# Low parts of three weight operands of the first feed-forward projection: an adding transfer in SBUF in place of a VectorE subtraction

## The chip, the cores and the metric

The kernel runs on one core of one Trainium2 chip. The metric is the device time of one execution in microseconds (us); the median of the runs counts. Engines are named as in the profile: PE is TensorE (its matmuls; PEld are its weight loads), DVE is VectorE, ACT is ScalarE, POOL is GpSimd, SP is SyncE, whose queue issues nearly all transfers.

## The reference, cut to what matters

One encoder layer over 2048 tokens of width 1024: windowed attention with a sink, then a SwiGLU feed-forward network of hidden width 2816, each between two RMS norms with shift, scale and gate from a conditioning vector. The change concerns the first product of the feed-forward network, `h @ w_in`.

```python
def swiglu(h, w_in, w_out):
    a, b = jnp.split(h @ w_in, 2, axis=-1)
    return (jax.nn.silu(a) * b) @ w_out

# in the layer:
    h = rmsnorm(x, ffn_norm_pre[i]) * (1.0 + sc2) + sh2
    y = swiglu(h, ffn_w_in[i], ffn_w_out[i])
    x = x + g2 * rmsnorm(y, ffn_norm_post[i])
```

All data is float32.

## The kernel before, in words

**Precision.** PE multiplies in a rounded format (`F32R`). To keep float32 accuracy each operand is held as a high part, the rounded value, and a low part, the operand less its high part. `three` (L876) issues three matmuls for one product: high by high, high by low, low by high. `split` (L882) makes the parts of an operand: ACT copies the operand into the rounded tile (`act.copy(hi, src)`), and then DVE subtracts (`lo = src - hi`).

**The first projection.** The tokens are done in two halves of 1024 (`hf`), and in each half the 44 column tiles of `w_in` in 22 pairs (`t`): the tile of `a` and that of `b` that belong together. One pair in one half is a `Hidden` block (L1540), so there are 44. A block is a 2 by 2 matrix product done by a scheme of seven products in place of eight. Its constructor, `Block.__init__` (L1490), loads the two weight tiles into `raw` (named `wiri` in the profile, 512 KB each), takes four quarters `a11, a12, a21, a22` from them, makes four sums and differences on DVE (`s1, s2, s4` as tiles of their own, `s3` over `a21`), and splits the seven operands `a11, s2, a12, s3, s1, a22, s4` into seven `w` tiles (L1511 to L1514), each of two times 128x512 elements. The profile names the tiles of `a11, a12, a22` together `wa_i`, those of the others `ws_i`. `step(i)` (L1518) then issues the 12 matmuls of one of the seven products (four slices of the contraction by `three`), 84 in a block. The activations' operands (`hb`, `ht`) are split once for each half.

**What comes of a product.** `take` (L1545) brings each product from its PSUM bank into the tiles `p1, u2, u3, b1`, on ACT for the first and on DVE for the others; ACT applies silu, POOL multiplies, and the results go to DRAM by SP for the second projection.

**Buffers.** There are two weight pools, used by even and odd blocks. Each has one `raw` tile and seven `w` tiles (`wbufs = 7`, L1458), so that operand `i` of block `t + 2` takes the place of operand `i` of block `t` once PE has used it.

**Order of the work.** No order is written by hand. `Recorder` (L142) records every operation with the regions that it reads and writes (`record`, L184) and a cost (`cost`, L256), and `schedule` (L702) makes the order of all engines from that: 18 rounds of a list schedule whose priorities come from a backward pass, of which it takes the one that does best under drawn lateness of transfers. So a change of one operation's cost or engine can move instructions everywhere, the attention included. What stands on an engine or a queue runs in its order; SP issues the transfers of loads and stores alike. All instructions are issued at one line of `emit`, L767 before and L771 after the change, so the profile is read by tile names.

**Around the start of the projection.** The last attention blocks store their output (`of`) to DRAM (`o_d`), from which the output projection of the last quarter of the tokens loads it as `ol`; its weights are `wo`. The first blocks' weights, the operands `hb` and `ht` and the normed activations (`y`, stored as `h2_d`, `hd_d`) are loaded, stored and split at the same time.

Of the kernel before, what the change touches and what calls it, by code (L numbers as in the profile page):

```python
# [16 lines left out]
AF = mybir.ActivationFunctionType  # L17
ALU = mybir.AluOpType
# [6 lines left out]
KT = D // P  # L25
# [116 lines left out]
class Recorder:  # L142
# [41 lines left out]
    def record(self, eng, fn, args, kw):  # L184
        op = Op()
        op.i, op.eng, op.fn, op.args, op.kw, op.ins = len(self.ops), eng, fn, args, kw, None
        aps = [(j, x) for j, x in list(enumerate(args)) + list(kw.items()) if isinstance(x, bass.AP)]
        out = {0}
        if fn == "custom":
            out = {1}  # L190
        elif fn == "tensor_tensor_reduce":
            out = {0, 7}
        elif fn == "activation" and "accum_out" in kw:
            out = {0, "accum_out"}
        op.writes = [self.region(x) for j, x in aps if j in out]
        op.reads = [self.region(x) for j, x in aps if j not in out]
        op.tiles = []
        if fn == "matmul" and not kw.get("start"):
            op.reads.append(op.writes[0])
        elif fn == "matmul" and op.writes[0][0].group is None:  # L200
            op.writes = [(op.writes[0][0], (3, (1 << P) - 1))]
        outs, ins = [x for j, x in aps if j in out], [x for j, x in aps if j not in out]
        op.forms, op.calls, op.stamp = {}, {}, 0
        for op.eng, op.fn, op.args, op.kw in (*self.others(eng, fn, args, kw, ins), (eng, fn, args, kw)):
            self.cost(op, outs, ins)
            op.forms[op.eng] = op.occ, op.lat, op.port, op.table
            op.calls[op.eng] = op.fn, op.args, op.kw
        op.eng_first = eng
        op.pred = {}
        for w, items in ((False, op.reads), (True, op.writes)):  # L210
            for b, m in items:
                for q, qw, qm in b.log:
                    if (w or qw) and q is not op and qm[0] & m[0] and qm[1] & m[1]:
                        op.pred[q] = max(op.pred.get(q, 0), self.gap(q, op))
        for w, items in ((False, op.reads), (True, op.writes)):
            for b, m in items:
                if w:
                    b.log = [e for e in b.log if not (e[2][0] | m[0] == m[0] and e[2][1] | m[1] == m[1]) or e[0] is op]
                b.log.append((op, w, m))
                if b.tag is not None and op not in b.ops:  # L220
                    if not b.ops:
                        b.tag.order.append(b)
                    b.ops.add(op)
                    op.tiles.append(b)
        if eng == "pe" and op.writes[0][0].group is not None:
            for q in op.writes[0][0].group:
                op.pred.setdefault(q, 0)
            op.writes[0][0].group = [op]
        op.succ = []
        for q in op.pred:  # L230
            q.succ.append(op)
        self.ops.append(op)
        return op
# [22 lines left out]
    def cost(self, op, outs, ins):  # L256
        fn, eng = op.fn, op.eng
        op.port, op.table, op.bytes = False, None, 0
        n = int(np.prod(outs[0].shape[1:])) if fn != "custom" else P
        sbuf = [x for x in ins if self.bufs[x.tensor.name].pool.space == "sbuf" and int(np.prod(x.shape[1:])) > 1] \  # L260
            if eng != "sp" else []
        psum = any(self.bufs[x.tensor.name].pool.space == "psum" for x in ins) if eng != "sp" else False
        if eng == "sp":
            op.bytes = int(np.prod(outs[0].shape)) * 4
            parts, run = outs[0].ap[0][1], min(self.run(x) for x in outs + ins)
            op.wire = op.bytes / (345.0 if run >= 2048 and parts == P else 270.0)
            op.occ, op.lat = 650 if parts == DH or run * 2 * P == op.bytes else 385 if run >= 2048 else 450, 0
            op.out = self.bufs[outs[0].tensor.name].pool.space == "dram"
        elif eng == "pe":
            if fn == "transpose":  # L270
                op.occ, op.lat = 108, 330
            elif outs[0].dtype == F32 and ins[0].dtype == F32:
                op.occ, op.lat = max(860 * n // CH, 230), max(1060 * n // CH, 400)
            else:
                op.occ = n * 0.4167 + 13.5
                op.lat = op.occ + 162
        elif eng == "act":
            op.occ = n / 1.2 + (51 if psum else 93)
            op.lat = op.occ + 105
            if fn == "activation":  # L280
                for more, ns in (("accum_out" in op.kw, 105), (isinstance(op.kw.get("scale"), bass.AP), 95),
                                 (isinstance(op.kw.get("bias"), bass.AP), 95)):
                    if more:
                        op.occ, op.lat = op.occ + ns, op.lat + ns
                f_ = op.args[2]
                op.table = {AF.Silu: "silu", AF.Ln: "log", AF.Exp: "log"}.get(f_)
        elif eng == "dve":
            fast = fn in ("tensor_copy", "tensor_scalar") and not psum
            op.occ = n / (1.92 if fast else 0.96) + 66
            op.lat = op.occ + 88  # L290
            if fn == "reciprocal":
                op.occ, op.lat = 90, 174
            if fn in ("tensor_tensor_reduce", "scalar_tensor_tensor") and any(
                    isinstance(x, bass.AP) and int(np.prod(x.shape[1:])) == 1 for x in op.args):
                op.occ, op.lat = op.occ + 62, op.lat + 62
            if fn == "tensor_tensor_reduce":
                op.lat += 84
            if outs[0].ap[0][1] == DH and fn == "tensor_tensor":
                op.occ, op.lat = op.occ + 97, op.lat + 10
            op.port = n > P and (fast or len(sbuf) > 1)  # L300
        else:
            op.port = fn != "custom"
            if fn == "tensor_tensor":
                op.occ = n * 2.21 + 125
                op.lat = op.occ + 45
            elif fn == "custom":
                op.occ, op.lat = 1000, 1050
            else:
                op.occ = n * 1.05 + 153
                op.lat = op.occ + 35  # L310
# [461 lines left out]
def f(ap):  # L772
    return ap.bitcast(F32)
# [14 lines left out]
def encoder_layer(ctx, tc, a):  # L788
# [697 lines left out]
    class Block:  # L1486

        STEPS = tuple(zip(("a11", "s2", "a12", "s3", "s1", "a22", "s4"), OPERANDS))

        def __init__(self, ops, i, u, wa, wb, keep=None, kept=None):  # L1490
            self.ops, self.u, m = ops, u, ops.m
            pl = wi[i % len(wi)]
            if kept:
                self.w = {}
                for n, _ in self.STEPS:
                    self.w[n] = w = pl.tile([P, 2, m, P], F32R, tag="w", bufs=wbufs, name=f"w{n}_{u}")
                    sp.dma_start(f(w), kept[n])
                return
            raw = pl.tile([P, 2, 2 * m, P], F32, tag="raw", name=f"wir{u}")
            sp.dma_start(raw[:, 0], wa)  # L1500
            sp.dma_start(raw[:, 1], wb)
            a11, a12, a21, a22 = [raw[:, i].rearrange("p (k e) c -> p e k c", e=2)[:, e] for i in range(2) for e in range(2)]
            sm_ = {n: pl.tile([P, m, P], F32, tag=n, name=f"{n}_{u}", bufs=1) for n in ("s1", "s2", "s4")}
            sm_["s3"] = a21
            dve.tensor_tensor(sm_["s1"], a21, a22, ALU.add)
            dve.tensor_tensor(sm_["s2"], sm_["s1"], a11, ALU.subtract)
            dve.tensor_tensor(sm_["s3"], a11, a21, ALU.subtract)
            dve.tensor_tensor(sm_["s4"], a12, sm_["s2"], ALU.subtract)
            src = dict(sm_, a11=a11, a12=a12, a22=a22)
            self.w = {}  # L1510
            for n, _ in self.STEPS:  # L1511
                w = pl.tile([P, 2, m, P], F32R, tag="w", bufs=wbufs, name=f"w{n}_{u}")
                split(w[:, 0], w[:, 1], src[n], dve)
                self.w[n] = w  # L1514
                if keep:
                    sp.dma_start(keep[n], f(w))
# [22 lines left out]

    class Hidden(Block):  # L1540
        def __init__(self, half, t, hf):
            super().__init__(half, t, f"i{half.u}_{t}", a["w_in"][t], a["w_in"][HT + t])
            self.t, self.got, self.hf = t, {}, hf

        def take(self, i, ps):  # L1545
# [377 lines left out]
```

## Time and profile before

| what | before |
|---|---|
| runs (us) | 2015.1, 2017.34, 2016.28; median 2016.28 |
| span of the profiled execution (us) | 2014.1 |
| PE busy (us, share of the span) | 1999.9, 99% |
| DVE busy | 1687.7, 84% |
| ACT busy | 1076.7, 53% |
| POOL busy | 559.6, 28% |
| DMA engines' mean busy share by packets of the main queue | 59.3% |
| matmuls | 9484 |

The profile gives the profiled execution by its span, from the first to the last instruction; a time of its own beside that is not given. The median of the runs lies 2016.28 - 2014.1 = 2.2 us above the span, the three runs 1.0 to 3.2 us above it. Busy times overlap, so they don't add up to the span. A matmul is recorded from its start to its modelled end, while the next starts before that end.

### The profile page before, as it was taken

The numbers are of one execution on the slowest core, as the hardware profiler recorded it, in microseconds if no ns is written. First come the engines' busy times: TensorE is split into PE (matmuls) and PEld (weight loads), VectorE is DVE, ScalarE is ACT, GpSimd is POOL, SyncE is SP. The second block draws the span as 40 slices with busy tenths as digits, with TensorE's granted clock in tenths as the row PEclk, the third lists the DMA queues.
The fourth block names the chain that finished last, engine by engine and source line by source line (L and its number), as shares of the span: only waits on it lengthen the run. The fifth ranks groups of instructions, "written<-read, shape, count | busy, mean of one in ns | idle before, by whom it ended". The sixth has DMA issues, their size and how long they took to land. (4 is left out here: it accounts for less than half of the span.)

```text
span 2014.1 us, 29137 instructions
## 1 busy us (share of the span) xinstructions
PE 1999.9 (99%) x9484; PEld 1675.3 (83%) x9484; DVE 1687.7 (84%) x3047; ACT 1076.7 (53%) x2100; POOL 559.6 (28%) x521
## 2 busy tenths in 40 slices
PE   9999999999999999999999999999999999999999
PEld 7888888888888788888888888888888888878888
DVE  7959888777989999988889988776676789989996
ACT  6657766777888863444343533333333744455433
POOL 0202433444757414332323211111111000130034
PEclk9999999999999999999999999999999999999999
DMA  9877655486788775444546833423323794398543
GB/s 350 303 281 279 225 201 188 171 302 218 239 290 288 270 274 177 172 174 157 193 161 230 286 128 126 142 89 110 110 95 126 244 322 150 113 322 302 174 155 111
DMA packets 208724, 415.23 MB, mean 206 GB/s; under 512 B 20107, under 2 KB 62140, under 8 KB 205500
## 3 DMA queue, kind: packets, MB, share of 16 engines
q1 hardware_dynamic: 208572, 413.37, 59.3%
q8 instruction: 75, 1.23, 0.3%
q14 instruction: 77, 0.63, 0.1%
HBM read 278.52 MB, written 134.77 MB: 205 GB/s over the span
## 5 line engine op out<-in xcount | busy, mean ns | idle before, releaser
L767 PE MATMUL bank<-ht,ws_i 128*128 128x512 f32 x1584 | 373.7, 389 | 0.0
L767 PEld LDWEIGHTS bank<-ht,ws_i 128*128 128x128 f32 x1584 | 297.4, 188 | 61.6
L767 PE MATMUL bank<-hb,wa_i 128*128 128x512 f32 x1056 | 255.2, 389 | 0.0
L767 PEld LDWEIGHTS bank<-hb,wa_i 128*128 128x128 f32 x1056 | 198.6, 188 | 41.2
L767 PE MATMUL bank<-ol,wo 128*128 128x512 f32 x768 | 207.2, 398 | 2.5 <-ACT ol L767 1.9
L767 DVE TENSOR_TENSOR u_i<-bank,u_i 128x512 f32<-128x512 f32 x176 | 120.8, 687 | 80.2 <-PE bank L767 79.2
L767 ACT ACTIVATE pr<-pr,nm 128x385 f32<-128x385 f32 (+1 forms) x256 | 154.8, 606 | 51.0 <-DVE nm L767 47.8
L767 ACT CAST ws_i<-s_i 128x512 fp32r<-128x512 f32 x132 | 82.0, 621 | 183.7 <-PE bank L767 147.2
L767 DVE CUSTOM_DVE_ANT_0 pr<-bank,bias,nsink 128x384 f32<-128x384 f32 (+1 forms) x256 | 150.0, 594 | 23.4 <-PE bank L767 19.6
L767 POOL TENSOR_SCALAR pr<-pr,rs 128x384 f32<-128x384 f32 (+1 forms) x184 | 116.6, 646 | 184.3 <-DVE rs L767 173.0
L767 PEld LDWEIGHTS bank<-ol,wo 128*128 128x128 f32 x768 | 142.4, 189 | 30.0 <-ACT ol L767 2.4
L767 POOL TENSOR_TENSOR p_i<-p_i,u_i 128x512 f32<-128x512 f32 x34 | 55.4, 1630 | 306.8 <-DVE u_i L767 187.8
L767 POOL TENSOR_TENSOR z<-z,z 128x512 f32<-128x512 f32 x31 | 49.6, 1611 | 327.3 <-DVE z L767 216.9
L767 PE MATMUL bank<-hi,ws 128*128 128x512 f32 x384 | 135.9, 399 | 0.0
L767 ACT CAST wa_i<-wiri 128x512 fp32r<-128x512 f32 x132 | 81.2, 620 | 101.0 <-PE bank L767 96.2
L767 DVE TENSOR_TENSOR plo<-bank,phi 128x512 fp32r<-128x512 f32 x184 | 121.1, 684 | 14.9 <-ACT phi L767 13.4
L767 PE MATMUL bank<-k,q 128*128 128x384 f32 (+1 forms) x512 | 132.7, 343 | 0.4 <-DVE nm L767 0.4
L767 PE MATMUL bank<-ht,wa_i 128*128 128x512 f32 x528 | 127.3, 389 | 0.0
L767 PE MATMUL bank<-hb,ws_i 128*128 128x512 f32 x528 | 127.1, 389 | 0.0
L767 DVE TENSOR_TENSOR z<-bank,z 128x512 f32<-128x512 f32 (+1 forms) x164 | 107.8, 659 | 16.9 <-PE bank L767 15.7
L767 ACT CAST phi<-bank 128x512 fp32r<-128x512 f32 x184 | 101.9, 587 | 29.0 <-PE bank L767 27.7
L767 DVE TENSOR_TENSOR wa_i<-wiri,wa_i 128x512 fp32r<-128x512 f32 x132 | 99.7, 756 | 20.9 <-ACT wa_i L767 20.9
(289 smaller groups left out, 4441.6 us busy)
## 6 DMA issues: line engine op xcount, KB each, us to landing
wiri<-w_in SPq DMA_DIRECT2D x88, 512.0 KB, 4.5
ada<-ada_w SPq DMA_DIRECT2D x38, 512.0 KB, 7.1
q_d<-e SPq DMA_DIRECT2D x32, 512.0 KB, 3.4
q<-q_d SPq DMA_DIRECT2D x16, 1024.0 KB, 6.8
wo<-wo_d SPq DMA_DIRECT2D x16, 1024.0 KB, 7.2
wiro<-w_out SPq DMA_DIRECT2D x40, 384.0 KB, 4.3
g_d_b<-p_i SPq DMA_DIRECT2D x44, 256.0 KB, 2.9
g_d_t<-p_i SPq DMA_DIRECT2D x40, 256.0 KB, 2.0
```

The costliest lines, as they stand in the source:

```text
L767: o.ins = getattr(engs[o.eng], o.fn)(*args, **kw)
```

## The change

For the three operands of a `Hidden` block that are plain quarters of the weights (`a11`, `a12`, `a22`), the low part is made in another way. ACT writes the high part as before. ACT also writes the operand times -1 into the low half of the tile, where it is rounded like the high part, so that it holds the negative high part. Then POOL issues a transfer from SBUF to SBUF that adds the operand to what the low half holds. The other four operands, and the blocks of the second projection, are split as before.

So that each quarter is one piece of 2 KB in a partition, the host lays `w_in` out with the even slices of the contraction first and the odd ones behind (`whole=True` selects the matching view). The recorder learns that such a transfer also reads what it writes, and it is costed at 1100 ns of POOL and 4500 ns to landing, without the port that POOL shares with DVE.

```diff
         if fn == "matmul" and not kw.get("start"):
+            op.reads.append(op.writes[0])
+        elif kw.get("accum_op") is not None:
             op.reads.append(op.writes[0])
...
-            op.port = fn != "custom"
-            if fn == "tensor_tensor":
+            op.port = fn not in ("custom", "dma_start")
+            if fn == "dma_start":
+                op.occ, op.lat = 1100, 4500
+            elif fn == "tensor_tensor":
...
-            a11, a12, a21, a22 = [raw[:, i].rearrange("p (k e) c -> p e k c", e=2)[:, e] for i in range(2) for e in range(2)]
+            form = "p (e k) c -> p e k c" if whole else "p (k e) c -> p e k c"
+            a11, a12, a21, a22 = [raw[:, i].rearrange(form, e=2)[:, e] for i in range(2) for e in range(2)]
...
-                split(w[:, 0], w[:, 1], src[n], dve)
+                if whole and n in ("a11", "a12", "a22"):
+                    act.copy(w[:, 0], src[n])
+                    act.activation(w[:, 1], src[n], AF.Copy, scale=-1.0)
+                    pool.dma_start(f(w[:, 1]), src[n], accum_op=ALU.add)
+                else:
+                    split(w[:, 0], w[:, 1], src[n], dve)
...
-            super().__init__(half, t, f"i{half.u}_{t}", a["w_in"][t], a["w_in"][HT + t])
+            super().__init__(half, t, f"i{half.u}_{t}", a["w_in"][t], a["w_in"][HT + t], whole=True)
...
-        "w_in": tiles(ffn_w_in[0]),
+        "w_in": tiles(ffn_w_in[0])[:, :, list(range(0, KT, 2)) + list(range(1, KT, 2))],
```

In the order of the instructions, 132 subtractions leave DVE (three for each of 44 blocks), and 132 activations on ACT and 132 transfers on POOL are new. The rest of the order is planned anew, and differs from the attention's first blocks on. Three places show it; a name such as `wa11_i0_0` is operand a11 of block 0 in the first half (`i1` is the second half), and the last number of a name only counts tiles.

PE, from the end of the attention to the first use of `ol3_3`, the last piece of attention output that is loaded; before, with three matmuls on `ol2_1` between the last attention product and the first row shown:

```order
L767 MATMUL bank1<-ol2_2_6066,wo2_7_7046 128x512 x6
L767 MATMUL bank1<-ol2_3_6097,wo2_7_7046 128x512 x6
L767 MATMUL bank0<-ol3_0_6624,wo3_0_7264 128x512 x6
L767 MATMUL bank0<-ol3_1_6924,wo3_0_7264 128x512 x6
L767 MATMUL bank0<-ol3_2_7231,wo3_0_7264 128x512
L767 MATMUL bank1<-ol3_0_6624,wo3_1_7367 128x512 x2
L767 MATMUL bank3<-hb110_0_7342,wa11_i0_0_7330 128x512
L767 MATMUL bank0<-ol3_2_7231,wo3_0_7264 128x512 x5
L767 MATMUL bank1<-ol3_0_6624,wo3_1_7367 128x512 x4
L767 MATMUL bank1<-ol3_1_6924,wo3_1_7367 128x512 x6
L767 MATMUL bank1<-ol3_2_7231,wo3_1_7367 128x512 x6
L767 MATMUL bank0<-ol3_3_7398,wo3_0_7264 128x512
```

The same stretch of PE after, with eleven matmuls on `ol2_0` and `ol2_1` between the last attention product and the first row shown:

```order
L771 MATMUL bank0<-ol2_2_6043,wo2_7_7110 128x512 x6
L771 MATMUL bank0<-ol2_3_6081,wo2_7_7110 128x512 x6
L771 MATMUL bank1<-ol3_0_6562,wo3_0_7240 128x512 x6
L771 MATMUL bank1<-ol3_1_6878,wo3_0_7240 128x512
L771 MATMUL bank0<-ol3_0_6562,wo3_1_7328 128x512 x2
L771 MATMUL bank1<-ol3_1_6878,wo3_0_7240 128x512 x4
L771 MATMUL bank3<-hb110_0_7346,wa11_i0_0_7338 128x512
L771 MATMUL bank1<-ol3_1_6878,wo3_0_7240 128x512
L771 MATMUL bank1<-ol3_2_7208,wo3_0_7240 128x512 x6
L771 MATMUL bank0<-ol3_0_6562,wo3_1_7328 128x512 x4
L771 MATMUL bank0<-ol3_1_6878,wo3_1_7328 128x512 x2
L771 MATMUL bank1<-ol3_3_7367,wo3_0_7240 128x512
```

With the matmuls named ahead of them, 52 matmuls stood between the last attention product and the first use of `ol3_3`; now 50 do. The first product that needs the low part of `wa11_i0_0` follows 21 matmuls behind that use.

POOL at the same time, before (`pr` is the attention's softmax, `y` and `yacc` belong to the norms):

```order
L767 TENSOR_SCALAR pr15_3_7111<-pr15_3_7111,rs15_3_7214 128x256 x4
L767 TENSOR_TENSOR y1_1_5399<-y1_1_5399,nx1_7150 128x512
L767 TENSOR_TENSOR y1_2_5559<-y1_2_5559,nx1_7150 128x512
L767 TENSOR_TENSOR y1_5_5977<-y1_5_5977,nx1_7150 128x512
L767 TENSOR_TENSOR y1_3_5676<-y1_3_5676,nx1_7150 128x512
L767 TENSOR_TENSOR y1_4_5793<-y1_4_5793,nx1_7150 128x512
L767 TENSOR_TENSOR y1_6_6000<-y1_6_6000,nx1_7150 128x512
L767 TENSOR_TENSOR yacc2_6299<-yacc2_6299,ysq2_7_7383 128x512
```

And after:

```order
L771 TENSOR_SCALAR pr15_3_7101<-pr15_3_7101,rs15_3_7153 128x256 x4
L771 TENSOR_TENSOR yacc2_6247<-yacc2_6247,ysq2_5_7223 128x512
L771 TENSOR_TENSOR y1_0_5285<-y1_0_5285,nx1_7264 128x512
L771 TENSOR_TENSOR y1_1_5397<-y1_1_5397,nx1_7264 128x512
L771 DMA wa11_i0_0_7338<-wiri0_0_6099 128x512
L771 TENSOR_TENSOR yacc2_6247<-yacc2_6247,ysq2_6_7311 128x512
L771 TENSOR_TENSOR y1_2_5538<-y1_2_5538,nx1_7264 128x512
L771 DMA wa12_i0_0_7362<-wiri0_0_6099 128x512
L771 TENSOR_TENSOR y1_5_5966<-y1_5_5966,nx1_7264 128x512
L771 TENSOR_TENSOR y1_4_5830<-y1_4_5830,nx1_7264 128x512
L771 TENSOR_TENSOR y1_7_6173<-y1_7_6173,nx1_7264 128x512
L771 TENSOR_TENSOR yacc2_6247<-yacc2_6247,ysq2_7_7379 128x512
```

The first two of block 0's three transfers stand among the norms of the second quarter, the third behind them. On SP, six transfers stood between the store of the last attention output and the load of `ol3_3`; now two do.

ACT in the middle of the second half (blocks 8 to 10), before:

```order
L767 COPY p1_i1_8_12480<-bank3 128x512
L767 CAST wa11_i1_10_12486<-wiri1_10_12312 128x512
L767 CAST ws2_i1_10_12502<-s2_i1_10_12378 128x512
L767 CAST wa12_i1_10_12520<-wiri1_10_12312 128x512
L767 ACTIVATE p1_i1_8_12480<-p1_i1_8_12480 128x512
```

And after:

```order
L771 COPY p1_i1_8_12575<-bank7 128x512
L771 ACTIVATE wa11_i1_10_12581<-wiri1_10_12435 128x512
L771 CAST wa11_i1_10_12581<-wiri1_10_12435 128x512
L771 CAST ws2_i1_10_12598<-s2_i1_10_12488 128x512
L771 ACTIVATE wa12_i1_10_12617<-wiri1_10_12435 128x512
L771 CAST wa12_i1_10_12617<-wiri1_10_12435 128x512
L771 ACTIVATE p1_i1_8_12575<-p1_i1_8_12575 128x512
```

In both, operand a11 of block 10 is copied directly behind the first product of block 8, which frees its tile; the new activation with -1 stands ahead of the copy. On SP, `wiri1_10` is loaded after block 8's a22 is done in both, after the change behind the landing of that block's three transfers.

More of the change, by code (lines that the diff above doesn't have):

```diff
@@ L1488, in encoder_layer, with __init__ @@
         STEPS = tuple(zip(("a11", "s2", "a12", "s3", "s1", "a22", "s4"), OPERANDS))
-        def __init__(self, ops, i, u, wa, wb, keep=None, kept=None):
+        def __init__(self, ops, i, u, wa, wb, keep=None, kept=None, whole=False):
             self.ops, self.u, m = ops, u, ops.m
```

## The prediction

> **What bounds the kernel now.** I read the page's busy times first, then the busy times stretch by stretch.
>
> ```profile
> core 0: us, PE busy (x) PEld busy (x) DVE busy (x) ACT busy (x) POOL busy (x), PEclk, DMA share, GB/s
> 100.00:650.00 550.00, 548.88 (x2902) 471.92 (x2901) 452.37 (x1095) 405.62 (x921) 241.15 (x292) 1.00 0.72 244
> ...
> 690.00:695.00 5.00, 2.54 (x9) 1.54 (x8) 2.79 (x4) 3.50 (x5) 0.68 (x1) 0.91 1.03 400
> 695.00:700.00 5.00, 5.00 (x18) 3.78 (x17) 4.00 (x6) 4.46 (x7) 0.00 (x0) 0.75 1.06 403
> 700.00:1560.00 860.00, 860.00 (x3796) 712.35 (x3795) 704.56 (x1040) 342.38 (x569) 206.39 (x135) 1.00 0.47 163
> ```
>
> The first projection runs from about 685 to 1564 us. Between 700 and 1560 PE is busy for all 860.00 us, at a granted clock of 1.00, with 3796 matmuls: one each 226.6 ns. Busy alone would not show a gap shorter than the overlap of two matmuls, so I looked for one in the pace:
>
> ```profile
> 1000.00:1050.00 50.00, 50.00 (x222) 41.40 (x222) 41.91 (x63) 21.91 (x34) 12.71 (x8) 1.00 0.49 166
> 1400.00:1450.00 50.00, 50.00 (x223) 41.40 (x222) 34.03 (x52) 15.84 (x26) 7.55 (x5) 1.00 0.29 101
> ```
>
> At 1000 us DVE is busy for 41.91 of 50 us, at 1400 us for 34.03, and the pace of PE is the same, 222 and 223 matmuls. So DVE sets nothing there. In the whole projection PE waits in one place, near its start. The waits of PE between 685 and 745 us, and the timeline around them:
>
> ```profile
> PE bank L767 <- ACT ol L767: 1.9, 1, 1.9
> PE bank L767 <- DVE ol L767: 0.5, 1, 0.5
> ```
>
> ```profile
> 678.05 0.42 PE L767 MATMUL bank<-plo,v 128*128 128x512 f32 x1
> ...
> 680.26 0.53 SPq L767 DMA_DIRECT2D o_d<-of  x1
> ...
> 684.78 0.32 SPq L767 DMA_DIRECT2D ol<-o_d  x1
> ...
> 691.14 1.04 ACT L767 CAST ol<-ol 128x1024 fp32r<-128x1024 f32 x1 [1.41 <-DMA ol<-o_d]
> ...
> 692.23 0.73 PE L767 MATMUL bank<-ol,wo 128*128 128x512 f32 x2 [1.93 <-ACT ol L767]
> ```
>
> The last attention product starts at 678.05, its output is stored at 680.26 and loaded again at 684.78, and ACT can copy it at 691.14; PE, out of other work, waits. From 690 to 700 us it does 9 + 18 = 27 matmuls where 10 us at 226.6 ns hold 44, in part at a clock of 0.75: 17 x 0.2266 = 3.9 us are lost. That is all the time near the change that can be won.
>
> **The change, part by part.** Rows of the operand tiles, then the group on the page:
>
> ```profile
> L767 ACT CAST wa_i<-wiri x132: 602/622/642, 678.1 to 1529.1; 128x512 fp32r<-128x512 f32 x132
> ```
>
> ```profile
> L767 DVE TENSOR_TENSOR wa_i<-wiri,wa_i 128x512 fp32r<-128x512 f32 x132 | 99.7, 756 | 20.9 <-ACT wa_i L767 20.9
> ```
>
> DVE loses 132 x 756 ns = 99.8 us. It lies wholly beside PE's 860.00 of 860 us, so it is worth 0; what is late next, with DVE gone, is PE itself, as it is now. ACT gains 132 copies with a factor; the nearest row is its plain copy, 622 ns, so 82 us on an engine that is busy for 342.38 of 860 us. It stays below half; 0. If that cover were gone, 82 us would be the price.
>
> POOL gains 132 issues. No transfer issued by POOL is in the trace. The nearest row is SP's issue of the same weights (327/423/1841 ns):
>
> ```profile
> L767 SPq DMA_DIRECT2D wiri<-w_in x88: 327/423/1841, 580.1 to 1492.7; - x88
> ```
>
> By these ends it is 43 to 243 us in all; I take the upper one, since POOL must make the transfer's list in some way, and 206 + 243 still leaves half of 860 us idle. Queued behind a POOL transfer that waits for ACT are POOL's products of the gated halves; they go to DRAM and are used a phase later. So 0.
>
> The landing is what a matmul now waits for. Transfers of the steady part, and of the crowded start (680 to 745 us):
>
> ```profile
> wiri<-w_in SPq DMA_DIRECT2D x36, 512.0 KB, 4.5
> g_d_t<-p_i SPq DMA_DIRECT2D x18, 256.0 KB, 2.0
> ```
>
> ```profile
> DMA packets 11364, 22.99 MB, mean 354 GB/s; under 512 B 1248, under 2 KB 1504, under 8 KB 11360
> ...
> ht<-hd_d_t SPq DMA_DIRECT2D x16, 256.0 KB, 5.8
> ...
> wor<-w_o SPq DMA_DIRECT2D x4, 512.0 KB, 6.8
> ```
>
> An adding transfer of 256 KB reads its source and its target, so it lies between the copy of 256 KB and of 512 KB: 2.0 to 4.5 us steady, 5.8 to 6.8 us at the start. I take the upper ends. The Trainium skill (Collectives: The Full Stack, "The bandwidth ceiling: the fold count and why AG ≠ RS ≠ AR") says that the adding itself is free, but that two sources are read, which makes twice the read traffic of a copy; it speaks against the change, and the sum by it is the upper end, by a plain copy the lower. No run of before shows such a transfer.
>
> How early it starts is told by the order of the instructions: operand i of block t + 2 is written when operand i of block t has been used. A block has 84 matmuls, 19.0 us, a product 12, 2.7 us. So from there to its own use lie 2 x 19.0 - 2.7 = 35.3 us, for two ACT operations (1.2 us), POOL's issue (1.8 at most) and the landing (4.5): 28 us of reserve. The other edge is the reload of the raw tile, which now waits in SP's queue for the landing, with stores of the gated results queued behind it. From the end of the sixth product of block t - 2 (a22 of t is written) to the end of the first of block t (a11 of t + 2 is written) lie 2.7 + 19.0 + 2.7 = 24.4 us; the reload takes at most 8.7:
>
> ```profile
> DMA to landing us min/median/max: 3.4/4.5/8.7
> ```
>
> 24.4 - 8.7 - 1.2 leaves 14.5 us for issue and landing before even a copy is late. So the steady part costs 0, and the new traffic has room: DMA's share there is 0.47. The relaid `w_in` changes the size of no load and the length of no operation: 0.
>
> At the start the sum is not 0. Three terms, at the wait on `ol`. (a) PE has 50 matmuls instead of 52 to fill it: +0.45 us. (b) SP has two transfers instead of six between the store and the load, and the store needed 684.78 - 680.26 = 4.5 us; a store in uncrowded queues lands in 2.0, so 0 to -2.5 us. (c) The first two adding transfers stand on POOL near there, and at 400 GB/s each fills the queues for 0.65 us (256 KB) to 1.3 us (512 KB): +1.3 to +2.6 if they fall between store and load, 0 if not. From -2.1 to +3.1, middle +0.5. The low part of `wa11_i0_0` itself is used 21 matmuls, 4.8 us, after the load has been waited for, and so has over 10 us to land. The six transfers of blocks 1 and 2 fill at most 6 x 1.3 = 7.8 us of a stretch at 354 GB/s; PE keeps its pace there, so 0, and 7.8 if its loads have no reserve.
>
> Last, the new order of the attention. Its PE is busy for 548.88 of 550 us, so 1.1 us can be won that the view shows, and short gaps under the overlap may go or come; the worst slice of the trace, 650 to 700 us, lost 2.9. I take 0, with an estimated 3 us either way from these two.
>
> Sum: 2014.1 (span) + 0 + 0.5 + 0 = 2014.6; the median of the runs lies 2.2 above the span, so **2016.8 us**, against 2016.28. No measurable change: what a measurement can tell is about 0.2%, 4.0 us.
>
> **The rivals.**
> *The start pays (slower).* The 9 adding transfers of blocks 0 to 2 enter queues that are full from 685 to 745 us; loads of `ol`, `wo`, `hb` and `ht` land later by what was put ahead of them, 9 x 0.65 to 9 x 1.3 = 5.9 to 11.7 us, and PE, which has just shown that it can run dry there, pays it. For it: shares of 1.03 and 1.06. Against it: from 700 us on PE didn't wait in just such queues, and only two transfers stand before the load that it waits for. It decides from 4 us of delay that reaches PE: 2016.3 + 8 = 2024 us. Chance 0.17.
> *The landing is late in every block (slower).* If issue and landing take over 14.5 us, the reload holds SP; over about 14.5 + 35 = 50 us, each pair of blocks is late by the rest. At 60 us, 22 x 10 = 220 us: 2236. Against it stand all landings quoted, 8.7 at most. Chance 0.04.
> *DVE's relief and the new order gain (faster).* The wait on `ol` goes, 3.9 us with the clock's dip, and the attention gains its 1.1 us: 2016.3 - 5.0 = 2011.3. For it: term (b). Against it: both must come, and term (a). Chance 0.13.
> That the change doesn't do what it says is no rival: the order has 132 transfers on POOL and 132 fewer subtractions on DVE.
>
> **How the numbers follow.** The forecast has 0.66; its own range is 2016.8 with -2.1 - 3 and +3.1 + 3, 2011.7 to 2022.9, the ends needing both terms at once. Low 2012: the faster rival lies below. High 2024 takes in the rival at the start up to its middle. Left out are about 0.1 below, 0.04 of the late landings and some 0.05 of the start's upper part. Of the forecast's 0.66 I give 0.02 to the far low end and 0.04 to the far high end. Faster by over 0.2%: 0.13 + 0.02 = 0.15. Slower: 0.17 + 0.04 + 0.04 = 0.25. Same: 0.60.
>
> **What would show it.** Right: 222 matmuls in each 50 us from 750 to 1540 us; DVE busy there lower by near 100 us, ACT higher by near 82; adding transfers that land within 7 us; PE's idle before `ol` 0.4 to 5.5 us. Wrong: PE waiting for a `wa_i` tile or its transfer, a slice of the projection with fewer than 220 matmuls, or several us gained or lost in the attention.

## The result and the profile after

The changed kernel takes **2027.26 us** (median of 4 runs, 2025.93 to 2031.17), the kernel before beside it 2016.54 (2015.10 to 2017.34): a ratio of 1.0060, 95% interval 1.0046 to 1.0074. It is slower by about 11 us, and outside the predicted range. Its profiled execution took 2025.93 us, with a span of 2024.1.

Busy times of the changed kernel, from the page, and its groups for the operand tiles:

```profile
PE 2003.5 (99%) x9484; PEld 1673.7 (83%) x9484; DVE 1624.2 (80%) x2964; ACT 1143.0 (56%) x2232; POOL 588.8 (29%) x604
...
L771 POOL DMA_DIRECT2D wa_i<-wiri x132 | 116.1, 881 | 490.9 <-ACT wa_i L771 386.5 <-DMA g_d_b<-u_i 43.5 <-PE bank L771 18.2
...
L771 ACT ACTIVATE wa_i<-wiri 128x512 fp32r<-128x512 f32 x132 | 83.3, 631 | 107.8 <-PE bank L771 99.8 <-DMA wiri<-w_in 7.8
```

The engines did what the change says: 132 activations of 631 ns on ScalarE, 132 issues of 881 ns on GpSimd, no subtraction of these tiles. Now the same stretches as in the prediction (span of the stretch, busy time and count of each engine, granted clock, DMA share, GB/s), changed kernel:

```profile
150.00:200.00 50.00, 47.86 (x234) 39.22 (x234) 42.91 (x99) 34.80 (x77) 10.63 (x15) 1.00 0.78 275
100.00:650.00 550.00, 545.53 (x2875) 466.09 (x2873) 447.11 (x1082) 401.51 (x910) 236.63 (x287) 1.00 0.70 239
...
705.00:710.00 5.00, 2.19 (x5) 1.82 (x6) 2.04 (x3) 2.95 (x5) 0.22 (x1) 0.76 1.03 313
710.00:715.00 5.00, 5.00 (x21) 4.04 (x20) 4.27 (x5) 3.92 (x7) 1.62 (x1) 0.89 1.02 360
...
1170.00:1180.00 10.00, 9.04 (x38) 6.66 (x37) 7.26 (x11) 5.75 (x10) 5.32 (x4) 1.00 1.03 341
1180.00:1570.00 390.00, 390.00 (x1722) 322.85 (x1721) 267.04 (x428) 156.66 (x276) 68.86 (x72) 1.00 0.58 155
...
1000.00:1050.00 50.00, 50.00 (x223) 41.30 (x222) 40.01 (x61) 21.33 (x37) 12.88 (x12) 1.00 0.68 190
1400.00:1450.00 50.00, 50.00 (x222) 41.42 (x221) 33.48 (x52) 19.96 (x35) 8.31 (x9) 1.00 0.52 139
```

From 1180 to 1570 us, and at 1000, TensorE keeps its pace of 222 or 223 matmuls in 50 us: the steady part is untouched. The losses are in three places. In the attention, 2875 matmuls from 100 to 650 us where before had 2902; the stretch from 150 to 200, with 47.86 busy, is the first of it, and nothing of the change is executed there: the first adding transfer starts at 689.5 us. At the start of the projection, 5 + 21 matmuls from 705 to 715 us where 10 us hold 44, with the clock granted at 0.76 and 0.89 behind the gap. And at the turn from the first half of the tokens to the second, 38 in 10 us.

Where that time goes is seen in four rows that stand in both kernels: the last matmul of the attention (`plo,v`), of the output projection (`ol,wo`, which runs into the start of the first projection), of the first projection with `ht` and a `wa_i` tile, and the first of the end (`z,ident`). Columns: count, shortest/median/longest in ns, start of the first and of the last. Before, then changed:

```profile
L767 PE MATMUL bank<-plo,v x184: 387/393/508, 178.7 to 678.1; 128*128 128x512 f32 x184
...
L767 PE MATMUL bank<-ol,wo x768: 387/389/632, 416.6 to 731.9; 128*128 128x512 f32 x192
...
L767 PE MATMUL bank<-ht,wa_i x528: 389/389/389, 743.7 to 1564.4; 128*128 128x512 f32 x176
```

```profile
L771 PE MATMUL bank<-plo,v x184: 387/393/499, 183.5 to 683.6; 128*128 128x512 f32 x184
...
L771 PE MATMUL bank<-ol,wo x768: 387/389/628, 421.2 to 740.7; 128*128 128x512 f32 x192
...
L771 PE MATMUL bank<-ht,wa_i x528: 389/389/389, 748.9 to 1576.3; 128*128 128x512 f32 x176
```

The changed kernel is late by 683.6 - 678.1 = 5.5 us at the end of the attention, by 740.7 - 731.9 = 8.8 at the start of the projection, by 1576.3 - 1564.4 = 11.9 at its end; at `z,ident` by 9.8 (2015.4 against 2005.6), as the end of the kernel gives a little back.

### The profile page after: what moved, and what is told of

It reads as the page before. It is cut to its first block, busy times and chain, and to the rows that moved or that the text cites. A ratio compares the mean times of both kernels' runs of the same rounds, so it can differ in the third digit from the quotient of the medians.

```text
span 2024.1 us, 29538 instructions
## 1 busy us (share of the span) xinstructions
PE 2003.5 (99%) x9484; PEld 1673.7 (83%) x9484; DVE 1624.2 (80%) x2964; ACT 1143.0 (56%) x2232; POOL 588.8 (29%) x604
## 3 DMA queue, kind: packets, MB, share of 16 engines
q1 hardware_dynamic: 208572, 413.37, 59.6%
q0 software_dynamic: 19008, 34.61, 9.5%
## 5 line engine op out<-in xcount | busy, mean ns | idle before, releaser
L771 POOL DMA_DIRECT2D wa_i<-wiri x132 | 116.1, 881 | 490.9 <-ACT wa_i L771 386.5
L771 PE MATMUL bank<-ol,wo 128*128 128x512 f32 x768 | 212.0, 399 | 0.8 <-DVE wo L771 0.4
L771 ACT ACTIVATE wa_i<-wiri 128x512 fp32r<-128x512 f32 x132 | 83.3, 631 | 107.8 <-PE bank L771 99.8
L771 DVE TENSOR_TENSOR plo<-bank,phi 128x512 fp32r<-128x512 f32 x184 | 121.4, 685 | 14.5 <-ACT phi L771 13.2
L771 PEld LDWEIGHTS bank<-hb,ws_i 128*128 128x128 f32 x528 | 98.9, 188 | 22.6 <-DVE hb L771 1.7
```

Of the source, the lines that this page charges most:

```text
L771: o.ins = getattr(engs[o.eng], o.fn)(*args, **kw)
```

## The experiments

Two theories stood at first. **Plan**: the planner's new order of the attention, not the new operations, took the time. **Transfers**: the adding transfers crowd the DMA queues, or come late. In the table further down, "start" is the start of the last `ol,wo` less that of the last `plo,v`, and "projection" that of the last `ht,wa_i` less that of the last `ol,wo`, so that a loss earlier does not enter. The traces have TensorE's 9484 matmuls in one and the same order in the changed kernel, e2, e5, e6, e7, e8 and e12, and in the order of before in e1, so that these can be compared place by place.

### The old order with the new operations, and the reverse

`e1_new_ops_old_order` plans as before and replaces at emission; `e2_old_ops_new_order` does the reverse, in the changed kernel's order.

```
# e1: planned as before; emitted (without the planner's waits between
#     engines that hang on these instructions)
 act.copy(w[:, 0], src[n])           -> the copy, then activation(w[:, 1], src[n], scale=-1.0)
 dve.tensor_tensor(w[:, 1], ...)     -> nc.gpsimd.dma_start(f(w[:, 1]), src[n], accum_op=ALU.add)
# e2: planned as changed; emitted
 act.copy, act.activation            -> one copy, at the first of the two places
 pool.dma_start(f(w[:, 1]), ...)     -> nc.vector.tensor_tensor(w[:, 1], src[n], f(w[:, 0]), ALU.subtract)
```

> The order of all instructions is that of before; only the 132 subtractions are replaced at their places by the activation with -1 (behind the copy) and the adding transfer. Against before, the changed kernel lost about 3.5 us at 195 us, in the attention, about 1 us more in the rest of the attention, 5 us between 700 and 745 us and 1.9 us at 1175 us. Theory 'the new plan': the new operations cost nothing by themselves, so this runs at 2016.5, within 2 us of before, and none of the four losses is there. Rival 'the new operations': the losses at 700 to 745 and at 1175 us come from the transfers and activations, so this runs at 2022 to 2024.

> The converse: the order of all instructions is that of the changed kernel, but the low parts are made by DVE as before, at the place of the transfers, without the activation with -1. Theory 'the new plan': 2025 to 2028, as the changed kernel, with all four losses. Rival 'the new operations': only the 4.5 us of the attention stay, 2020 to 2022.

Measured: e1 **2041.06** (ratio 1.0125, 1.0112 to 1.0138), e2 **2022.65** (1.0034, 1.0022 to 1.0046). Neither theory had e1: put where ScalarE's copy and VectorE's subtraction stood, the new operations together cost 25 us. e2 came just above the 2020 to 2022 us of its rival. The timeline of e1 where TensorE first stands still in the projection (start, duration, engine, instruction, and in brackets the idle time before it and what ended it):

```profile
837.09 0.81 SPq L773 DMA_DIRECT2D wiri<-w_in  x2
...
838.89 0.48 SPq L773 DMA_DIRECT2D ly<-y_d  x1
...
839.85 0.88 POOL L769 DMA_DIRECT2D wa_i<-wiri  x1 [3.93 <-ACT wa_i L775]
...
841.93 0.87 POOL L769 DMA_DIRECT2D wa_i<-wiri  x1 [1.20 <-ACT wa_i L775]
...
846.65 0.69 DVE L773 TENSOR_TENSOR ly<-ly,lr 128x512 f32<-128x512 f32 x1 [5.38 <-DMA ly<-y_d]
...
849.14 0.63 ACT L773 ACTIVATE xsq<-ly 128x512 f32<-128x512 f32 x1 [6.58 <-DVE ly L773]
...
849.68 0.57 ACT L773 COPY p_i<-bank 128x512 f32<-128x512 f32 x1
...
850.30 1.22 PE L773 MATMUL bank<-hb,ws_i 128*128 128x512 f32 x2 [3.85 <-ACT p_i L773]
```

The load of `ly` is issued at 838.89 with a weight reload just ahead of it and two adding transfers behind it, and VectorE can use it only near 846.6, 7.8 us later. VectorE stands at that instruction for 5.38 us; ScalarE's square of `ly` stands behind VectorE; the copy that empties a PSUM bank (`p_i<-bank`) stands behind the square; and TensorE waits 3.85 us for the bank. Between 760 and 1120 us `ly` lands in 5.1 us (median) in e1, in 3.5 before. TensorE's waits for a transfer's own tile come to 2.3 us in all of e1. So the transfers harm less by their own landing than by what they make late, and the engines' queues carry that to TensorE where an order has no reserve for it. This is one of e1's stops, read off its trace; that all 25 us are of this kind was not shown. e2 says that the new order without a transfer, with the old subtractions put into it, costs about 7 us, so both theories hold a part; some 4 of these 7 us turn out below to be the subtractions' place in that order.

### Other orders of the same operations

```
-SPARE = 800.0
+SPARE = 810.0     # e3 (before), e4 (changed); 790.0 in e9 (before), e10 (changed)
```

`SPARE` is the reserve that the planner asks of loads; every operation stays, the order is another.

> The kernel before, with the planner's reserve for transfers at 810 ns in place of 800 (about half of the rows of PE's order change, the operations don't). Theory 'the new plan': plans of the same operations differ by several us, so this may lie 3 to 10 us off before, either way. Rival 'the new operations': a new plan alone is worth little, 2014.5 to 2018.5.

> The changed kernel with the reserve at 810 ns. Theory 'the new plan': it comes off 2027 by 3 to 10 us, most likely downwards, and the loss at 195 us goes or moves. Rival 'the new operations': it stays at least 5 us above the replanned kernel before, at 2021 or more.

> The kernel before with the planner's reserve at 790.0 instead of 800.0: the same operations in a second other order. Theory that the order alone moves the time by several us, and that the kernel before has one of the better orders: 2018 to 2026 us (with the reserve at 810.0 it took 2021.95). Rival, that one replanning was an unlucky one and the order is worth nothing: 2014 to 2017 us.

> The changed kernel with the planner's reserve at 790.0 instead of 800.0: the new operations in a third order. If the transfers cost about 4 us beyond the order in every plan, this lies about 4 us above the kernel before planned with the same reserve, and in all at 2021 to 2031 us. Rival, that orders made for the transfers can be as good as that of before: 2014 to 2018 us.

> The changed kernel once more, unaltered, for its place beside these three on the same chip: 2025 to 2029 us by what it took first (2027.26). If it takes 2021 to 2023 here, the 4.6 us put down to the transfers in this order would be the scatter of its runs.

| reserve | before | changed |
|---|---|---|
| 790 | 2022.87 (2020.86 to 2024.98) | 2025.07 (2021.07 to 2025.55) |
| 800 (as in the kernels) | 2015.38 to 2016.54 by batch | 2027.26; again 2027.31 (2023.22 to 2029.66) |
| 810 | 2021.95 (2021.11 to 2023.05) | 2025.49 (2021.08 to 2031.63) |

The kernel before has the best of its three orders, by 2021.95 - 2015.51 = 6.4 and 2022.87 - 2015.38 = 7.5 us, as the theories of e3 and e9 had it; those of the changed kernel lie within 2.3 us of each other. With the reserve at 790 and 810 the new operations cost 2025.07 - 2022.87 = 2.2 and 2025.49 - 2021.95 = 3.5 us, not 11, though the runs overlap. So e4 met neither of its forecasts: it came off the changed kernel's time by 1.8 us, not 3 to 10, and lies less than 5 us above e3. In e10 the rival (an order as good as that of before) failed, and the distance was nearer 2 than the 4 us that were forecast. The median of e12 repeats the first time of the changed kernel, so its distance to e2 is not the scatter of one set of runs; but its single runs spread over 6 us.

### Where a transfer costs

All of these but the last keep the changed kernel's order.

```
# e5: the activation by -1 stays; in place of the transfer
+ nc.vector.tensor_tensor(w[:, 1], src[n], f(w[:, 1]), ALU.add)
# e6: in 8 of the 44 blocks as e2; the other 108 transfers stay
+ CROWD = {(0, 0), (0, 1), (0, 2), (0, 3), (0, 20), (0, 21), (1, 0), (1, 1)}   # (hf, t)
# e7: the reverse of e6: only the 24 transfers of CROWD stay
# e8: all transfers, as plain copies
+ kw.pop("accum_op", None)
# e11: as e6, but the planner is told, and makes its own order
+ if whole and not self.split and n in ("a11", "a12", "a22"):   # self.split = (hf, t) in CROWD
```

> The changed kernel's own order, with the activation by -1 kept on ScalarE, and VectorE adding the operand onto the negative high part at the place where GpSimd issued the adding transfer; there is no adding transfer left. Theory that the transfers cost by their time in the DMA queues (the changed kernel stands 4.6 us above the same order with the old subtraction, 2022.65): the time is that of the old subtraction, 2022 to 2024 us. Rival, that the 132 more activations on ScalarE cost it: 2026 to 2028 us, as with the transfers.

> The changed kernel's own order; in 8 of the 44 blocks (the first four of the first half, its last two, the first two of the second half, where the DMA engines are full) the low parts are made by VectorE's subtraction as before, at the place of the transfer, without the activation by -1; the other 36 blocks keep the 108 adding transfers. Theory that the transfers cost only where the DMA engines are full already: 2022 to 2024 us. Rival, that each transfer costs its share of the 4.6 us: 4.6 x 108/132 = 3.8 us above 2022.65, so 2026 to 2027 us.

> The changed kernel's own order; only the 8 blocks in which the DMA engines are full keep the 24 adding transfers (the first four of the first half, its last two, the first two of the second half), the 36 others make the low parts by VectorE's subtraction as before. Theory that the transfers cost where the DMA engines are full: 2026 to 2028 us. Rival, that each transfer costs its share: 4.6 x 24/132 = 0.8 us above 2022.65, so 2023 to 2024 us.

> The changed kernel's own order with the same 132 transfers, but copying the operand over the low part instead of adding it (so the low parts are not those of the reference); each transfer then has one source instead of two. Theory that the second source is what the queues pay for: the software queue's time per byte falls from 1.9 times to about once that of the hardware queue, its share of the span from 9.5% to about 5%, and the time by about half of the 4.6 us, to 2023.5 to 2025.5 us. Rival, that the cost is the issue on GpSimd and the wait for any transfer: 2026 to 2028 us.

> The planner knows that the 8 blocks at the start of the projection, at the end of its first half and at the start of its second (where the DMA engines are full) keep VectorE's subtraction, and makes its own order for that; 36 blocks have the adding transfers. Theory, transfers cost only where the DMA engines are full: no loss against the order's own luck, 2015 to 2023 us, and no wait of TensorE for a load or a ScalarE copy behind one between 700 and 745 us over 2 us. Rival, that transfers cost in every block: 2024 to 2030 us.

| kernel | us, median | ratio to before (95%) | start | projection |
|---|---|---|---|---|
| before | 2016.35 | | 53.8 | 832.5 |
| changed | 2027.26 | 1.0060 (1.0046 to 1.0074) | 57.1 | 835.6 |
| e12, changed again | 2027.31 | 1.0061 (1.0046 to 1.0077) | 57.8 | 833.7 |
| e2, no transfer, no activation by -1 | 2022.65 | 1.0034 (1.0022 to 1.0046) | 52.1 | 837.9 |
| e5, no transfer | 2023.13 | 1.0034 (1.0022 to 1.0047) | 51.6 | 838.1 |
| e6, 108 transfers | 2020.98 | 1.0025 (1.0015 to 1.0034) | 52.7 | 833.9 |
| e7, the other 24 | 2024.03 | 1.0041 (1.0027 to 1.0055) | 55.1 | 835.2 |
| e8, plain copies | 2020.18 | 1.0021 (1.0012 to 1.0030) | 53.2 | 833.1 |
| e11, as e6, own order | 2016.46 | 1.0004 (0.9995 to 1.0013) | 53.4 | 832.9 |

Each ratio is to the runs of the kernel before that were taken beside it; "start" and "projection" are those of one profiled execution each. e5 rules ScalarE's additional work out in this order: with it and without transfers the time is that of e2. e6 has 82% of the transfers and is faster than e5, which has none, and than its own forecasts; against the changed kernel its time says that the 24 transfers of the crowded blocks cost about 6 us. e7, which has only those 24, shows the loss at the start (55.1 against 51.6 and 52.7), but its whole time is just 1.4 us above e2, as its rival had it. The places tell why the two don't add up. e5 and e2 lose time in the projection (838.1 and 837.9 us) where the changed kernel, e6 and e7 lose none, around 851 us; TensorE of e5 and its one wait there:

```profile
851.36 0.49 PE L773 MATMUL bank<-nhil,ones 128*128 128x512 f32 x1 [1.25 <-DVE nhil L773]
852.61 0.47 PE L773 MATMUL bank<-nlol,ones 128*128 128x512 f32 x1 [0.76 <-issue]
```

This order was made with VectorE relieved, and at that place has no room for the old subtractions. VectorE writes `nhil` at 850.33 us in e2, at 850.89 in e5 and at 851.63 in e7, which is no earlier; but TensorE, late from the start, comes to that product only at 853.76 in e7, and finds it there. So e2 and e5 lose some 4 us that e7 does not, and e7 less e2 says too little of the transfers at the start; the order alone is worth less than the 7 us of e2.

The wait at the start, in the same order of the same instructions. Waits of TensorE between 685 and 745 us, then of SyncE between 690 and 710, then GpSimd's transfers and the issues of SyncE; the changed kernel first:

```profile
PE bank L771 <- ACT hb L771: 2.9, 1, 2.9
```

```profile
SPq L771 <- DMA hd_d_t<-hf: 3.0, 1, 3.0
SPq L771 <- DMA hd_d_t<-y: 1.8, 1, 1.8
```

```profile
689.47 1.05 POOL L771 DMA_DIRECT2D wa_i<-wiri  x1
...
693.73 0.87 POOL L771 DMA_DIRECT2D wa_i<-wiri  x1
...
703.68 0.88 POOL L771 DMA_DIRECT2D wa_i<-wiri  x1
```

```profile
690.79 1.65 SPq L771 DMA_DIRECT2D hd_d_t<-hf  x1
...
700.93 0.32 SPq L771 DMA_DIRECT2D ht<-hd_d_t  x1
703.18 0.32 SPq L771 DMA_DIRECT2D hb<-h_d  x1
...
707.05 0.62 ACT L771 CAST hb<-hb 128x512 fp32r<-128x512 f32 x1 [3.24 <-DMA hb<-h_d]
...
707.81 0.76 PE L771 MATMUL bank<-hb,wa_i 128*128 128x512 f32 x1 [2.90 <-ACT hb L771]
```

And e6, in which blocks 0 to 3 have no transfer:

```profile
SPq L779 <- DMA hd_d_t<-y: 0.9, 1, 0.9
SPq L779 <- DMA hd_d_t<-hf: 0.7, 1, 0.7
```

```profile
693.53 0.32 SPq L779 DMA_DIRECT2D hd_d_t<-hf  x1
...
700.04 0.32 SPq L779 DMA_DIRECT2D ht<-hd_d_t  x1
701.33 0.32 SPq L779 DMA_DIRECT2D hb<-h_d  x1
...
705.83 0.62 ACT L779 CAST hb<-hb 128x512 fp32r<-128x512 f32 x1 [0.52 <-DMA h_d<-y]
...
706.60 0.47 PE L779 MATMUL bank<-hb,wa_i 128*128 128x512 f32 x1
```

The store `hd_d_t<-hf` lands late: the load `ht<-hd_d_t`, which must wait for it at the head of SyncE's queue, is issued 8.5 us after the end of the store's issue, in e6 6.2 us. SyncE waits 3.0 us there instead of 0.7, and then 1.8 instead of 0.9 for a second store, `hd_d_t<-y`, which took 9.8 us to land, in e6 6.8. The load of `hb` stands behind these, and TensorE waits 2.9 us for its split. The second run of the changed kernel, e12, has the same: SyncE waits 2.5 and 1.7 us, TensorE 3.3. In e7 SyncE's wait for `hd_d_t<-hf` is 3.3 us and TensorE's 2.3, in e8 1.7 and 1.6, in e5 0.8 and 0.2. So it is the adding transfers, and the issues tell which: ahead of these waits GpSimd has issued only the first two of block 0, at 689.47 and 693.73, which take 9.1 us to land (median). The third follows at 703.68, behind the issue of the `hb` load; those of blocks 1 and 2 come from 743 us on.

At the turn the changed kernel waits for `hb` in two small gaps, 9.04 of 10 us busy. But its second run e12 is busy for 10.00 there, as e5, e6, e7 and e8 are, and its projection is 833.7 us, not 835.6; so this loss of some 1.8 us comes in one run and not in another, and what of it is due to the transfers is not shown.

e8 tells what of a transfer it is. DMA queues (packets, MB, share of 16 engines' span) of the changed kernel, then of e8, and the landing at the start (690 to 760 us) in each:

```profile
q1 hardware_dynamic: 208572, 413.37, 59.6%
q0 software_dynamic: 19008, 34.61, 9.5%
...
wa_i<-wiri POOLq DMA_DIRECT2D x7, 256.0 KB, 6.3
```

```profile
q1 hardware_dynamic: 208572, 413.37, 59.2%
q0 software_dynamic: 10560, 34.61, 4.3%
...
wa_i<-wiri POOLq DMA_DIRECT2D x8, 256.0 KB, 4.2
```

For the same 34.61 MB the adding takes 9.5 / 4.3 = 2.2 times the engines' time of the copying, and the time of the kernel falls by 7 us without it, more than the 2 to 4 us that were expected; it lies below e2 and e5 too, since it does not lose the 4 us at 851. The adding also makes 144 packets of a transfer where the copy makes 80, so that the second source and the smaller packets are not told apart.

e11 is the plainest answer. Left alone in the first blocks, the planner drew the order of the kernel before again: by the tile names of the traces TensorE's matmuls differ in 4 of 9484 places, all in the seventh block, and ScalarE's and SyncE's instructions are the same to about 750 us. So its attention and its start are those of before, and beyond that 108 adding transfers run in an order made for them. Its waits of TensorE and its rows:

```profile
PE bank L771 <- ACT ol L771: 2.0, 1, 2.0
PE bank L771 <- DVE plo L771: 1.1, 1, 1.1
...
PE bank L771 <- ACT hb L771: 0.6, 1, 0.6
```

```profile
L771 PE MATMUL bank<-plo,v x184: 387/393/499, 178.7 to 678.0; 128*128 128x512 f32 x184
...
L771 PE MATMUL bank<-ol,wo x768: 387/389/504, 416.6 to 731.4; 128*128 128x512 f32 x192
...
L771 PE MATMUL bank<-ht,wa_i x528: 389/389/390, 743.1 to 1564.3; 128*128 128x512 f32 x176
```

It is back at the old wait for `ol` and at 2016.46 us, as its theory had it. Against before that is no difference that can be measured; it does not beat it either, since TensorE has nothing more to give there.

With e6 and e11 the loss can be taken apart: they hold the same operations, 108 transfers in the same blocks, in two orders. Taking the ratios to before: e11 1.0004, that is 0.8 us for 108 transfers outside the crowd in an order made for them; e6 less e11, 0.0021, 4.2 us for the changed kernel's order; changed less e6, 0.0060 - 0.0025 = 0.0035, 7.1 us for the 24 transfers in the crowd. By the intervals the first is uncertain by about 2 us, the second by 2.5, the third by 3.5. The 7.1 holds with the other 108 in place, and it is a median over runs that spread by 5 us: the two profiled ones show 4.4 and 5.1 us of it at the start and 1.7 and none in the projection; where the rest falls in the longer runs is not shown.

## Why the prediction was wrong

**The failed steps are two.** The first is term (c): the first two adding transfers were priced only by the time that they fill the queues, and only at the wait on `ol`, "+1.3 to +2.6 if they fall between store and load, 0 if not". They were paid at another wait. Two stores that were under way with them landed late, SyncE's queue stood behind these, and TensorE waited 2.9 us for `hb` and then ran at a lower clock. The start grew from 53.8 to 57.1 us, by 4.4 against e6 and by 5.1 in the second run, where the whole sum of the start had +0.5. That TensorE did not wait in crowded queues before was taken as reserve; it showed only that this order fitted those queues. The step that says this outright, "The six transfers of blocks 1 and 2 fill at most 6 x 1.3 = 7.8 us of a stretch at 354 GB/s; PE keeps its pace there, so 0, and 7.8 if its loads have no reserve", is not where the loss came from: those six were issued from 743 us on, after it. The rival *The start pays* had this mechanism, with a chance of 0.17 and 8 us as its price, but for nine transfers, where two were enough.

**The second**: "Last, the new order of the attention", taken as "0, with an estimated 3 us either way". It was 4.2 us (e6 against e11); in the seven profiled runs of the new order the last attention product starts at 682.2 to 685.3 us, in the three of the old order at 677.9 to 678.1. So the term was not 0, and its size lay at or beyond the edge of the 3 us. The estimate was drawn from the gaps of one order, and these say how well that order came out, not what another would be. Every kernel with another order of the attention, with the old operations (e2, e3, e9) or the new, was 4 to 12 us slower than before; an order with 548.88 of 550 us busy has little left to win and much to lose.

What held: VectorE's relief was worth nothing; by the page it fell by 63.5 us over the whole kernel, less than the 99.8 worked out, since the planner gave it 49 other operations (3047 - 132 + 49 = 2964), products of the gated halves among them that GpSimd gave up for its issues. ScalarE's new row is 83.3 us, against 82 worked out. The issues on GpSimd, 116.1 us, lay between the bounds 43 and 243. The steady part is 0: 222 matmuls in 50 us, and 0.8 us for 108 transfers in e11, which can't be told from 0. The landing, 4.5 us taken for the steady part and 6.8 for the start, came out at 4.6 over all and 6.3 at the start, but the first two took 9.1 (7.8 in e12; medians of the two), beyond the 7 that the prediction named as its sign; the rival of a landing late in every block, which needed 14.5 for issue and landing, has nothing for it:

```profile
DMA to landing us min/median/max: 3.2/4.6/9.2
```

The wait for `ol` fell from 1.9 to 0.4 us, within 0.4 to 5.5 counted as idle there, as the term (b) allowed; what it gave was lost again at `hb`, some 12 us later. The Trainium skill (Collectives: The Full Stack, "The bandwidth ceiling: the fold count and why AG ≠ RS ≠ AR") says that the reducing step of a collective reads two sources and so makes twice the read traffic of a copy. The trace of this adding transfer agrees in size: 9.5 / 34.61 against 59.6 / 413.37 is 1.9 times the engines' time per byte of the other transfers, though what of it the smaller packets cost is not told apart. The prediction had this in its bounds and spent it only on the transfer's own landing and on the wait for `ol`, where the start shows that other transfers paid it.

## What to carry to other kernels

Price a transfer that is added not only by its own landing, but by what it makes late in the stretch where the queues are fullest: find there the in-order queue that waits for a landing, and who stands behind it. A move of work that hides in a steady part can be had at no cost that was measured if the crowded stretches at its ends are left as they were, as e11 did. And where a planner sets the order, a change of any operation draws a new order everywhere: plan the unchanged kernel anew two or three times before judging, since here that alone moved the time by 6.4 and 7.5 us.

## What the runs showed of the hardware that was not expected

An adding transfer of 256 KB within SBUF made 19008 / 132 = 144 packets and cost 2.2 times the queue time of a copying one with 80. Over all 132 the adding ones landed in 4.6 us and the copying ones of e8 in 2.9 (medians). GpSimd's issue of an adding one took 0.87 us (847 to 1187 ns), of a copying one 0.54 (538 to 739), where SyncE's issues of the weight loads had a median of 0.42. With the transfers, the stores of the gated halves `g_d_t<-p_i` landed in 5.0 us instead of 2.0 (medians between 760 and 1540 us). And around TensorE's 2.9 us wait the granted clock was at 0.76 and 0.89 in two stretches of 5 us, so that the gap cost more than its own length: 44 - 26 = 18 matmuls of 226.6 ns, 4.1 us.
